# The attention sink of a hybrid decoder kernel as a 129th score column instead of a separate operand

## The chip, the cores and the metric

The kernel runs on one core of a Trainium2 chip. The metric is the device time of one execution in microseconds (us); lower is better. Engines are named as in the profile: PE is TensorE's matrix multiplication and PEld its weight load, DVE is VectorE, ACT is ScalarE, POOL is GpSimd, SP is SyncE, whose queue issues nearly all DMAs.

## What is computed

A trunk of two layers on 512 tokens of width 1024. Each layer has two branches side by side, a gated DeltaNet (8 heads, chunks) and a sliding-window attention (16 query heads on 2 key heads, head width 64, window 128), then an output projection and an MLP of width 4096. The part that the change touches is the attention's softmax with a learned sink per head:

```python
    sink = sinks.astype(jnp.float32).reshape(SW_KV_HEADS, G)[None, None, :, :, None, None]
    m = jnp.maximum(jnp.max(scores, axis=-1, keepdims=True), sink)
    p = jnp.exp(scores - m)
    probs = p / (jnp.sum(p, axis=-1, keepdims=True) + jnp.exp(sink - m))
```

The sink takes part in the maximum and in the sum, and has no value row of its own.

## The kernel before

All large products are done three times over in a split of float32 into a high and a low part (`fp32r`): high by high, low by high, high by low (L339 to L341, L359 to L361, L387 to L389, L400 to L404). Weights come in chunks of 128x1024 by a DMA on SP's queue (`load`, L274), ACT makes the high part (L323) and DVE the low part (L324); `LOOK` = 4 chunks are made ahead and 5 raw buffers are held.

A layer is one long stream of work that a scheduler orders per engine when the program is built: it takes instructions by their place in the program and by its own estimate of when their inputs and buffers are ready, so instructions of different units stand mixed in an engine's queue. Each engine then runs its queue strictly in that order. Only where the program says so (`Order`) is an order written out by hand; of the attention that holds for the four transposes of a group (L919 to L923).

The attention runs in 16 groups per layer (L948), one for each of 4 blocks of 128 tokens (t), 2 key heads (g) and 2 halves (e), and each group has 4 query heads (j). The loop at L959 to L978 issues, for each group, first the units of `MIX` (L46: projections K, G and A of 24 matmuls of 512 columns each; a K unit also does a 128x128 product per chunk and DVE work at L740 to L752), then the first half of `att_group` (L870), then the second half of the group before. In this way a group's softmax has a whole projection unit of matmuls beside it.

First half of a group: scores on PE into PSUM `ps_s` (L892, L893); for t = 0 DVE adds the mask into `M` (L895), else ACT copies the older block's scores (L899) and DVE overwrites those in the band (L900), so that `M` holds 4 heads x 128 scores per token; DVE takes the negated maximum per head (L904, `nm`), the minimum with the negated sink (L905), the difference of the two (L907, `es`); ACT takes exp of that (L908), then four times exp of 128 scores with the row's sum (L910, `den`); DVE adds `es` to `den` (L912) and inverts it (L913); ACT scales the four parts (L916). Second half: four transposes on PE (L922), high part on ACT and low part on DVE (L411, L412 through `split`), two triangular selects on POOL (L932), the product with the values (L938), and the result into `qt` (L941 on ACT, L942 on DVE).

`M` is a 128x512 tile of the pool `T[2]` with four buffers. The negated sinks `nsk` are made once a layer from `snk` (L624 to L628, a DMA on SP and two small DVE instructions). POOL's other work at this time is the rotary embedding (L826 to L831), one power of 128x4 in each K unit (L744), and the selects.

Of the kernel before, what the change touches and what calls it, by code (L numbers as in the profile page):

```python
# [10 lines left out]
F32 = mybir.dt.float32  # L11
# [3 lines left out]
AF = mybir.ActivationFunctionType  # L15
ALU = mybir.AluOpType
AX = mybir.AxisListType
# [3 lines left out]
P = 128  # L21
# [98 lines left out]
def hybrid_trunk(ctx, tc, x, positions, pre_mix_g, dn_conv_w, dn_a_log, dn_dt_bias, dn_norm_g,  # L120
                 sw_sinks, post_mix_g, pre_mlp_g, post_mlp_g, wpk, out, depth=2, dump=None):
    nc = tc.nc
    x = x.rearrange("b s d -> (b s) d")
    out = out.rearrange("b s d -> (b s) d")
# [5 lines left out]
    sm = ctx.enter_context(tc.tile_pool(name="sm", bufs=2))  # L130
# [4 lines left out]
    mm, tr = nc.tensor.matmul, nc.tensor.transpose  # L135
    act, stt = nc.scalar.activation, nc.vector.scalar_tensor_tensor
    tt, ts = nc.vector.tensor_tensor, nc.vector.tensor_scalar
# [3 lines left out]
    def pool_of(tag, bufs):  # L141
        def get(name, dt=F32, n=512):
            return up.tile([P, n], dt, name=name, tag=tag, bufs=bufs)
        return get

    def s1(name, n):
        return sm.tile([P, n], F32, name=name, bufs=1)

    US = pool_of("s", 8)
    T = [pool_of(f"t{i}", 4) for i in range(8)]  # L150
# [8 lines left out]
    def PS(name):  # L159
        return pp.tile([P, 512], F32, name=name, tag="ps")  # L160
# [4 lines left out]
    def PZ(name):  # L165
        return pp.tile([P, 512], F32, name=name, tag="ss", bufs=2)
# [24 lines left out]
    def c4(ap):  # L191
        return ap.rearrange("p (c i) -> p c i", c=4)


    ident = const.tile([P, P], F32, name="ident")
# [214 lines left out]
    def split(src, hi, lo):  # L410
        nc.scalar.copy(hi, src)  # L411
        tt(out=lo, in0=src, in1=hi.bitcast(F32), op=ALU.subtract)  # L412

    def pair(U, name):
        return U(name + "_h", F32R), U(name + "_l", F32R)
# [104 lines left out]
    for l in range(depth):  # L520
# [89 lines left out]
        ps = PS("ps_cw")  # L610
# [11 lines left out]
        dma(dtb, dn_dt_bias[l].partition_broadcast(P))  # L622
        snk = s1("snk", QH)
        dma(snk, sw_sinks[l].partition_broadcast(P))  # L624
        nsk = sm.tile([P, 2, 2, 4], F32, name="nsk", bufs=1)
        for g in range(2):
            ts(out=nsk[:, g], in0=snk[:, g * 8:(g + 1) * 8].rearrange("p (j e) -> p e j", e=2),
               scalar1=-1.0, scalar2=None, op0=ALU.mult)  # L628

        x_res = x if l == 0 else xd  # L630

# [15 lines left out]
        for t in range(NT):  # L647
# [10 lines left out]
           in1=dtb.unsqueeze(2).broadcast_to([P, H, NC]), op=ALU.add)  # L658
# [157 lines left out]
        def att_rope(t):  # L816
            cos, sin = cs[:, t, 0, :], cs[:, t, 1, :]
            for a, nh in ((qt[t], QH), (kv[t][:, 0:128], 2)):
                v = a.rearrange("p (h d) -> p h d", d=HD)
                x1, x2 = v[:, :, 0:HALF], v[:, :, HALF:ROT]  # L820
                cb = cos.unsqueeze(1).broadcast_to([P, nh, HALF])
                sb = sin.unsqueeze(1).broadcast_to([P, nh, HALF])
                rt = T[7]("rt")
                tm = [rt[:, i * P:i * P + nh * HALF].rearrange("p (h d) -> p h d", d=HALF)
                      for i in range(4)]
                ptt(out=tm[0], in0=x1, in1=cb, op=ALU.mult)  # L826
                ptt(out=tm[1], in0=x2, in1=sb, op=ALU.mult)
                ptt(out=tm[2], in0=x2, in1=cb, op=ALU.mult)
                ptt(out=tm[3], in0=x1, in1=sb, op=ALU.mult)
                ptt(out=x1, in0=tm[0], in1=tm[1], op=ALU.subtract)  # L830
                ptt(out=x2, in0=tm[2], in1=tm[3], op=ALU.add)  # L831
# [24 lines left out]
        def att_q(t, g):  # L856
            ps = PS("ps_q")
            for i in range(4):
                j = g * 4 + i
                tr(ps[:, i * P:(i + 1) * P], qt[t][:, j * P:(j + 1) * P], ident)  # L860

            for e in range(2):
                a = T[7]("qT", F32R)
                rh, rl = slice(e * HD, (e + 1) * HD), slice((1 - e) * HD, (2 - e) * HD)
                act(out=a[rh], in_=ps[rh], func=AF.Copy, scale=HD ** -0.5)
                stt(out=a[rl], in0=ps[rh], scalar=HD ** -0.5, in1=a[rh].bitcast(F32), op0=ALU.mult,
                    op1=ALU.subtract)
                at["q", e] = a

        def att_group(t, g, e):  # L870

            if g == 0 and e == 0:
                if t == 0:
                    att_rope(0)
                att_prep(t)
            if (g, e) == (1, 0) and t < NT - 1:
                att_rope(t + 1)
            if e == 0:
                att_q(t, g)
            w0 = max(t - 1, 0) * P  # L880
            qh, den = at["q", e], sm.tile([P, 4], F32, name="den", bufs=4)
            kTh, kTl = kT[g]
            M = T[2]("M")
            for jj in range(2):
                ps = PZ("ps_s")
                pv = ps.rearrange("p (j w) -> p j w", j=2)
                nw = P if t == 0 else 2 * P
                for j in range(2):
                    qs = slice((jj * 2 + j) * P, (jj * 2 + j + 1) * P)
                    kw = slice(w0, w0 + nw)  # L890
                    o_ = pv[:, j, 0:nw]
                    mm(o_, lhsT=qh[:, qs], rhs=kTh[:, kw], start=True, stop=False)  # L892
                    mm(o_, lhsT=qh[:, qs], rhs=kTl[:, kw], start=False, stop=True)  # L893
                Mv = c4(M)[:, jj * 2:jj * 2 + 2, :]
                if t == 0:  # L895
                    tt(out=Mv, in0=pv[:, :, 0:P], in1=ban.unsqueeze(1).broadcast_to([P, 2, P]),
                       op=ALU.add)
                    continue
                nc.scalar.copy(Mv, pv[:, :, 0:P])  # L899
                nc.vector.copy_predicated(  # L900
                    out=Mv, mask=ge.bitcast(I32).unsqueeze(1).broadcast_to([P, 2, P]),
                    data=pv[:, :, nw - P:nw])
            nm = sm.tile([P, 4], F32, name="nm", bufs=4)
            nc.vector.tensor_reduce(out=nm, in_=c4(M), axis=AX.X, op=ALU.max, negate=True)  # L904
            tt(out=nm, in0=nm, in1=nsk[:, g, e, :], op=ALU.min)  # L905
            es = sm.tile([P, 4], F32, name="es", bufs=4)
            tt(out=es, in0=nm, in1=nsk[:, g, e, :], op=ALU.subtract)  # L907
            act(out=es, in_=es, func=AF.Exp)  # L908
            for j in range(4):
                act(out=M[:, j * P:(j + 1) * P], in_=M[:, j * P:(j + 1) * P], func=AF.Exp,  # L910
                    bias=nm[:, j:j + 1], accum_out=den[:, j:j + 1])
            tt(out=den, in0=den, in1=es, op=ALU.add)  # L912
            nc.vector.reciprocal(den, den)  # L913
            for j in range(4):
                js = slice(j * P, (j + 1) * P)
                act(out=M[:, js], in_=M[:, js], func=AF.Copy, scale=den[:, j:j + 1])  # L916
            yield
            ps = PS("ps_pt")
            together = Order(nc.tensor)  # L919
            together.begin()  # L920
            for j in (3, 0, 1, 2):
                tr(ps[:, j * P:(j + 1) * P], M[:, j * P:(j + 1) * P], ident)  # L922
            together.end()  # L923
            pf = pair(T[3], "pf")
            split(ps, *pf)


            pvs = [(at["v", max(t - 1, 0)], 0, a) for a in pf]
            if t > 0:
                for a in pf:  # L930
                    b = T[6]("pc", F32R)
                    nc.gpsimd.affine_select(out=c4(b), in_=c4(a), pattern=[[0, 4], [1, P]],  # L932
                                            compare_op=ALU.is_ge, fill=0.0, base=0,
                                            channel_multiplier=-1)
                    pvs.append((at["v", t], 256, b))
            po = PS("ps_o")
            for i, (v_, o_, a) in enumerate(pvs):
                mm(po, lhsT=v_[:, o_ + g * P:o_ + (g + 1) * P], rhs=a, start=i == 0,  # L938
                   stop=i == len(pvs) - 1)
            o_ = qt[t][e * HD:(e + 1) * HD, g * 512:(g + 1) * 512]  # L940
            nc.scalar.copy(o_, po[HD:P])  # L941
            tt(out=o_, in0=po[0:HD], in1=o_, op=ALU.add)  # L942
# [16 lines left out]
        for i in range(16):  # L959
# [10 lines left out]
            g = att_group(*groups[i])  # L970
# [239 lines left out]
        for m in range(KT):  # L1210
            ps = PM("ps_us")
# [41 lines left out]
        for m in range(4):  # L1253
            ps = (PM, PM, PS, PZ)[m]("ps_ud")
            first.append((ps, mm_a(ps, yT, range(6))))
        mT = []
        for m in range(KT):
# [9 lines left out]
            if m < 4:  # L1267
                ps = first[m][0]
                mm_a(ps, yT, range(6, KT), first[m][1])
            else:  # L1270
                ps = PM("ps_ud")
# [15 lines left out]
        for t in range(NT):  # L1287
            ps = pss[t]
# [72 lines left out]
        for s in range(3):  # L1361
            left = {f"P{i}": [] for i in range(1, 8)}
            raw = [None, None]
            for i, m in enumerate(FF_ORDER):
                if s == 0 and i < 4:
                    ps = early[i][0]
                else:
                    ps = PM("ps_f1")
# [45 lines left out]
        for m in range(8):  # L1414
            ps = PM("ps_f1")
# [21 lines left out]
        else:  # L1437
            for t in range(NT):
                ps = PM("ps_f2")
# [26 lines left out]
```

## Time and profile before

| | us |
|---|---|
| median of 3 runs (1829.16 to 1831.1) | 1830.95 |
| the profiled execution's own time | 1830.59 |
| its span, first to last instruction | 1828.6 |
| PE busy / PEld busy | 1809.1 / 1503.9 |
| DVE busy / ACT busy / POOL busy | 1292.1 / 940.9 / 211.2 |

Busy times are unions of the intervals in which an engine had an instruction under way. Matmuls are pipelined and their ends are modelled, so PE shows as busy over short pauses too; a weight load (PEld) precedes each matmul and its records show such pauses. A wait is put down to the instruction whose semaphore came last.

### The profile page before, as it was taken

Reading aid. Unit: us, or ns where it says so; the run is one execution under the profiler, and the core shown is the slowest. Engines: PE = TensorE matmul, PEld = TensorE weight load, DVE = VectorE, ACT = ScalarE, POOL = GpSimd, SP = SyncE. Lnnn points to the kernel's source line nnn. Section 1 sums busy time; section 2 is a strip of 40 time slices with the busy share of each in tenths; the row PEclk is TensorE's granted clock in tenths of the full one; section 3 lists DMA queues with packets and bytes.
Section 4 is the critical chain, followed back from the end, with each engine's and each line's share of the span. In section 5 each row is a group of like instructions: output and inputs, shape, how many; then the busy total and the mean of one; then the engine's idle time right before and its main releaser. Section 6 shows DMA issues by size and latency. Waiting matters only on the chain.

```text
span 1828.6 us, 26748 instructions
## 1 busy us (share of the span) xinstructions
PE 1809.1 (99%) x9598; PEld 1503.9 (82%) x9598; DVE 1292.1 (71%) x2466; ACT 940.9 (51%) x1913; POOL 211.2 (12%) x386
## 2 busy tenths in 40 slices
PE   9999999999999999999999999999999999999998
PEld 8888778888788888888898887888887898888886
DVE  5499796887566758684556997968885568585934
ACT  6678742444434645544347877234444346554442
POOL 0322102221101000000003221022111010000000
PEclk9999999999999999999999999999999999999999
DMA  5633447554453363564245343485545534544631
GB/s 188 202 118 116 115 149 223 179 170 149 124 191 124 96 216 120 168 217 151 93 151 181 104 127 110 167 234 165 160 139 153 172 119 135 174 163 148 233 102 46
DMA packets 146422, 278.48 MB, mean 152 GB/s; under 512 B 33569, under 2 KB 66657, under 8 KB 146290
## 3 DMA queue, kind: packets, MB, share of 16 engines
q1 hardware_dynamic: 145778, 276.75, 47.4%
q8 instruction: 75, 1.23, 0.3%
q14 instruction: 57, 0.47, 0.1%
q0 software_dynamic: 512, 0.03, 0.0%
HBM read 239.38 MB, written 37.36 MB: 151 GB/s over the span
## 4 chain that ended last, share of the span: by engine, by line
PE 84%; DVE 6%; ACT 5%; DMA 3%; issue 1%; POOL 1%; SPq 0%; POOLq 0%; DVEq 0%; ACTq 0%
PE ps_f L340 6%; PE ps_f L339 6%; PE ps_f L341 6%; PE ps_p L402 3%; PE ps_p L404 3%; PE ps_p L400 3%; PE ps_b L388 3%; PE ps_b L387 3%; PE ps_b L389 3%; PE ps_vp L339 2%; PE ps_us L339 2%; PE ps_ud L339 2%; PE ps_vp L341 2%; PE ps_ud L341 2%; PE ps_ud L340 2%; PE ps_us L340 2%
## 5 line engine op out<-in xcount | busy, mean ns | idle before, releaser
L323 ACT CAST wh<-wr 128x1024 fp32r<-128x1024 f32 (+1 forms) x332 | 343.1, 1040 | 542.2 <-PE ps_f L340 145.8
L324 DVE TENSOR_TENSOR wl<-wr,wh 128x1024 fp32r<-128x1024 f32 (+1 forms) x332 | 400.4, 1216 | 303.6 <-ACT wh L323 300.6
L339 PE MATMUL ps_f<-g_h,wh 128*128 128x512 f32 x448 | 174.3, 389 | 0.0
L340 PE MATMUL ps_f<-g_l,wh 128*128 128x512 f32 x448 | 174.3, 389 | 0.0
L341 PE MATMUL ps_f<-g_h,wl 128*128 128x512 f32 x448 | 174.3, 389 | 0.0
L402 PE MATMUL ps_p<-wl,P_h 128*128 128x512 f32 x336 | 131.4, 391 | 0.4 <-DVE wl L324 0.3
L404 PE MATMUL ps_p<-wh,P_l 128*128 128x512 f32 x336 | 130.8, 389 | 0.0
L400 PE MATMUL ps_p<-wh,P_h 128*128 128x512 f32 x336 | 129.5, 389 | 0.0
L437 POOL TENSOR_TENSOR pr<-pq,pw 128x1 f32<-128x1 f32 x16 | 9.8, 613 | 807.6 <-DVE pq L436 807.6
L339 PEld LDWEIGHTS ps_f<-g_h,wh 128*128 128x128 f32 x448 | 84.1, 188 | 17.4
L341 PEld LDWEIGHTS ps_f<-g_h,wl 128*128 128x128 f32 x448 | 84.1, 188 | 17.4
L340 PEld LDWEIGHTS ps_f<-g_l,wh 128*128 128x128 f32 x448 | 84.1, 188 | 17.4
L402 PEld LDWEIGHTS ps_p<-wl,P_h 128*128 128x128 f32 x336 | 63.1, 188 | 15.8 <-DVE wl L324 2.4
L400 PEld LDWEIGHTS ps_p<-wh,P_h 128*128 128x128 f32 x336 | 63.1, 188 | 13.3
L404 PEld LDWEIGHTS ps_p<-wh,P_l 128*128 128x128 f32 x336 | 63.1, 188 | 12.8
L387 PE MATMUL ps_b<-wh,h_h 128*128 128x432 f32 (+1 forms) x192 | 71.1, 370 | 0.0
L388 PE MATMUL ps_b<-wl,h_h 128*128 128x432 f32 (+1 forms) x192 | 70.5, 367 | 0.3 <-DVE wl L324 0.3
L389 PE MATMUL ps_b<-wh,h_l 128*128 128x432 f32 (+1 forms) x192 | 70.2, 366 | 0.0
L293 DVE TENSOR_TENSOR wr<-wr 128x1024 f32<-128x1024 f32 x48 | 58.0, 1220 | 2.6 <-DMA wr<-in_weights_dram 1.9
L340 PE MATMUL ps_qp<-h_l,wh 128*128 128x512 f32 x128 | 54.0, 422 | 0.0
L339 PE MATMUL ps_vp<-h_h,wh 128*128 128x512 f32 x128 | 53.9, 421 | 0.0
L341 PE MATMUL ps_vp<-h_h,wl 128*128 128x512 f32 x128 | 53.6, 419 | 0.0
(359 smaller groups left out, 4873.6 us busy)
## 6 DMA issues: line engine op xcount, KB each, us to landing
wr<-in_weights_dram SPq DMA_DIRECT2D x320, 512.0 KB, 3.5
wr<-in_weights_dram SPq DMA_DIRECT2D x24, 432.0 KB, 3.6
D<-dd SPq DMA_DIRECT2D x32, 256.0 KB, 3.2
xd<-xo SPq DMA_DIRECT2D x12, 512.0 KB, 2.8
xt<-xd SPq DMA_DIRECT2D x24, 256.0 KB, 3.7
D<-gd SPq DMA_DIRECT2D x16, 256.0 KB, 6.5
dd<-D SPq DMA_DIRECT2D x16, 256.0 KB, 3.9
kkd<-kk SPq DMA_DIRECT2D x16, 256.0 KB, 2.0
```

The source lines that it names most:

```text
L293: tt(out=held[j], in0=held[j], in1=part(i, k, j), op=ALU.add)
L323: nc.scalar.copy(wh[:, :w], wr[:, :w])
L324: sub(out=wl[:, :w], in0=wr[:, :w], in1=wh[:, :w].bitcast(F32), op=ALU.subtract)
L339: mm(ps, lhsT=wh[:, k, :], rhs=hi, start=k == 0, stop=False)
L340: mm(ps, lhsT=wh[:, k, :], rhs=lo, start=False, stop=False)
L341: mm(ps, lhsT=wl[:, k, :], rhs=hi, start=False, stop=k == KT - 1)
L387: mm(pss[t], lhsT=hi[:, tsl], rhs=wh[:, r, :], start=k == 0, stop=False)
L388: mm(pss[t], lhsT=hi[:, tsl], rhs=wl[:, r, :], start=False, stop=False)
L389: mm(pss[t], lhsT=lo[:, tsl], rhs=wh[:, r, :], start=False, stop=k == KT - 1)
L400: mm(pss[t], lhsT=hi[:, c], rhs=wh[:, r, :], start=first, stop=False, skip_group_check=onto)
L402: mm(pss[t], lhsT=hi[:, c], rhs=wl[:, r, :], start=False, stop=False, skip_group_check=onto)
L404: mm(pss[t], lhsT=lo[:, c], rhs=wh[:, r, :], start=False, stop=last, skip_group_check=onto)
```

## The change

`M` gets 129 columns per head. POOL copies the group's four sinks into column 128 ahead of the scores; the maximum (L904) and the four exps with their sums (L910) run over 129 columns, so `nm` and `den` contain the sink. The minimum (L905), the difference (L907), its exp (L908) and the addition (L912) go, and so do `nsk` (L625 to L628) and `es`. The scaling and the transposes take the first 128 columns of each head.

```diff
-        nsk = sm.tile([P, 2, 2, 4], F32, name="nsk", bufs=1)
-        for g in range(2):
-            ts(out=nsk[:, g], in0=snk[:, g * 8:(g + 1) * 8].rearrange("p (j e) -> p e j", e=2),
-               scalar1=-1.0, scalar2=None, op0=ALU.mult)
...
-            M = T[2]("M")
+
+            M = T[2]("M", n=4 * (P + 1)).rearrange("p (j w) -> p j w", j=4)
+            nc.gpsimd.tensor_copy(M[:, :, P], snk[:, g * 8 + e:(g + 1) * 8:2])
...
-                Mv = c4(M)[:, jj * 2:jj * 2 + 2, :]
+                Mv = M[:, jj * 2:jj * 2 + 2, 0:P]
...
-            nc.vector.tensor_reduce(out=nm, in_=c4(M), axis=AX.X, op=ALU.max, negate=True)
-            tt(out=nm, in0=nm, in1=nsk[:, g, e, :], op=ALU.min)
-            es = sm.tile([P, 4], F32, name="es", bufs=4)
-            tt(out=es, in0=nm, in1=nsk[:, g, e, :], op=ALU.subtract)
-            act(out=es, in_=es, func=AF.Exp)
+            nc.vector.tensor_reduce(out=nm, in_=M, axis=AX.X, op=ALU.max, negate=True)
             for j in range(4):
-                act(out=M[:, j * P:(j + 1) * P], in_=M[:, j * P:(j + 1) * P], func=AF.Exp,
-                    bias=nm[:, j:j + 1], accum_out=den[:, j:j + 1])
-            tt(out=den, in0=den, in1=es, op=ALU.add)
+                act(out=M[:, j], in_=M[:, j], func=AF.Exp, bias=nm[:, j:j + 1], accum_out=den[:, j:j + 1])
             nc.vector.reciprocal(den, den)
             for j in range(4):
-                js = slice(j * P, (j + 1) * P)
-                act(out=M[:, js], in_=M[:, js], func=AF.Copy, scale=den[:, j:j + 1])
+                act(out=M[:, j, 0:P], in_=M[:, j, 0:P], func=AF.Copy, scale=den[:, j:j + 1])
...
-                tr(ps[:, j * P:(j + 1) * P], M[:, j * P:(j + 1) * P], ident)
+                tr(ps[:, j * P:(j + 1) * P], M[:, j, 0:P], ident)
```

## Rows read from the trace of the kernel before

**Rows 1.** The page: span, busy time of each engine, granted clock in 40 slices.

```profile
span 1828.6 us, 26748 instructions
...
PE 1809.1 (99%) x9598; PEld 1503.9 (82%) x9598; DVE 1292.1 (71%) x2466; ACT 940.9 (51%) x1913; POOL 211.2 (12%) x386
...
PEclk9999999999999999999999999999999999999999
```

**Rows 2.** Busy time by engine: layer 1's attention, an MLP stretch, layer 2's attention.

```profile
80.00:240.00 160.00, 157.48 (x810) 127.58 (x809) 138.56 (x408) 125.66 (x376) 34.33 (x58) 1.00 0.36 110
540.00:700.00 160.00, 159.79 (x812) 136.17 (x811) 102.77 (x129) 83.77 (x135) 5.67 (x8) 1.00 0.41 136
985.00:1145.00 160.00, 157.12 (x811) 127.49 (x810) 137.99 (x407) 125.32 (x373) 35.10 (x60) 1.00 0.36 111
```

Columns: from:to, length, then busy us and instructions of PE, PEld, DVE, ACT, POOL, then PE's granted clock, DMA share, GB/s.

**Rows 3.** Waits for the scaled scores: whole span, then from 80 to 240 us.

```profile
PE ps_pt L922 <- ACT M L916: 3.9, 6, 0.8
...
PEld ps_pt L922 <- ACT M L916: 9.5, 15, 1.2
...
PE ps_pt L922 <- ACT M L916: 2.0, 3, 0.8
```

Columns: who waited for whom: us in total, times, longest us.

**Rows 4.** Timeline of one group's softmax (the third of layer 1), DVE, ACT, PE.

```profile
101.92 0.68 DVE L904 TENSOR_REDUCE nm<-M 128x4 f32<-128x512 f32 x1
...
102.72 0.16 DVE L905 TENSOR_TENSOR nm<-nm,nsk 128x4 f32<-128x4 f32 x1
...
103.01 0.16 DVE L907 TENSOR_TENSOR es<-nm,nsk 128x4 f32<-128x4 f32 x1
...
103.60 0.19 ACT L908 ACTIVATE es<-es 128x4 f32<-128x4 f32 x1
103.70 0.39 ACT L910 ACTIVATE M<-M,nm 128x128 f32<-128x128 f32 x1
...
104.98 0.16 DVE L912 TENSOR_TENSOR den<-den,es 128x4 f32<-128x4 f32 x1 [0.21 <-ACT M L910]
...
105.73 1.28 ACT L916 ACTIVATE M<-M,den 128x128 f32<-128x128 f32 x4 [0.59 <-DVE cj L747]
...
107.06 0.66 PE L922 MATMUL ps_pt<-ident,M 128*128 128x128 f32 x4 [0.75 <-ACT M L916]
```

**Rows 5.** DVE and ACT by group of instructions: the ones removed.

```profile
L907 DVE TENSOR_TENSOR es<-nm,nsk 128x4 f32<-128x4 f32 x32 | 6.0, 188 | 0.1
L905 DVE TENSOR_TENSOR nm<-nm,nsk 128x4 f32<-128x4 f32 x32 | 5.9, 185 | 0.2
...
L912 DVE TENSOR_TENSOR den<-den,es 128x4 f32<-128x4 f32 x32 | 5.0, 157 | 7.2 <-ACT M L910 7.2
...
L908 ACT ACTIVATE es<-es 128x4 f32<-128x4 f32 x32 | 6.2, 195 | 1.3 <-DVE es L907 1.1
```

Columns: line, engine, operation, out<-in with shapes, count | busy us, mean ns of one | idle us before it and what ended it.

**Rows 6.** Durations of two lines of DVE: reads 1 to 3 elements off, and aligned.

```profile
L714 DVE SCALAR_TENSOR_TENSOR kk<-ps_kp,cw,kk x48: 717/741/751, 87.2 to 1085.4; 128x509 f32<-128x509 f32 x16, 128x510 f32<-128x510 f32 x16, 128x511 f32<-128x511 f32 x16
...
L718 DVE SCALAR_TENSOR_TENSOR kk<-th,kk x16: 656/691/695, 90.4 to 1087.6; 128x512 f32<-128x512 f32 x16
```

Columns: line, engine, operation, out<-in, count: shortest/median/longest ns, first and last start in us; shapes.

**Rows 7.** Small instructions of POOL, and the selects, by group.

```profile
L213 POOL MEMSET pw<- 128x4 f32 x1 | 0.1, 97 | 0.0
...
L830 POOL TENSOR_TENSOR kv<-rt 128x16 f32<-128x16 f32 x8 | 3.8, 481 | 0.2
...
L932 POOL TENSOR_SCALAR_AFFINE_SELECT pc<-pf_h 128x512 fp32r<-128x512 f32 x24 | 16.2, 675 | 122.9 <-ACT pf_h L411 122.9
```

**Rows 8.** Timeline: a select on POOL and a small DVE instruction beside it.

```profile
151.48 0.64 POOL L932 TENSOR_SCALAR_AFFINE_SELECT pc<-pf_h 128x512 fp32r<-128x512 f32 x1 [5.16 <-ACT pf_h L411]
...
151.52 0.61 DVE L742 TENSOR_SCALAR ssk<-ssk 128x4 f32<-128x4 f32 x1
```

**Rows 9.** The sinks' DMA and the waits of SP's queue for weight buffers.

```profile
L624 SPq DMA_DIRECT2D snk<-in_sw_sinks_dram x2: 328/328/328, 12.7 to 19.6; - x2
...
SPq L274 <- DVE wl L324: 641.6, 212, 13.2
```

Columns of the first: count, shortest/median/longest ns, start of the first and the last in us.

## The prediction

> **What bounds the kernel.** The page comes first: of a span of 1828.6 us PE is busy 1809.1, at full clock in every slice [rows 1]. So time changes only where PE's order of work gets a pause shorter or longer; work removed from DVE or ACT is worth nothing by itself. The second view is busy time by stage, for the two stretches in which the 16 attention groups of a layer run, with an MLP stretch beside them [rows 2]. By PE's own column the attention stretches have 160 - 157.48 = 2.5 and 160 - 157.12 = 2.9 us of idle time, 5.4 in all. DVE is the busiest of the others there, 138.56 and 137.99 of 160 (87%), against 102.77 in the MLP stretch: the softmax's small instructions stand in a queue that is nearly full.
>
> PE's column hides short pauses, since its ends are modelled. The weight loads show them: 136.17 us of loading in the MLP stretch against 127.58 and 127.49 in the attention, for nearly the same number of instructions [rows 2]. The differences are 8.6 and 8.7 us, 17.3 in all. Part of that is another mix of shapes, so I take 17.3 as an upper bound on what PE loses in both stretches and 5.4 as a lower one. The Trainium skill ("Trainium Kernel Development and Optimization", section Performance Expectations) says that matmul busy time is a bad measure and that the share of LDWEIGHTS is a good one; by that rule alone the room is 17.3 and not 5.4. No term of the forecast rests on it; it weighs only in the second rival.
>
> The third view is the waits. PE waits for the end of a group's scaling six times, 3.9 us in all and 0.8 at most, and PEld 15 times for 9.5 [rows 3]. Three of the six lie in the first layer, so three in the second, and they sum to 2.0 us in the first [rows 3]. One of them is written out in the timeline [rows 4]: maximum at 101.92, minimum with the sink at 102.72, difference at 103.01, exp of the sink at 103.60 between the first and the second exp of the scores, addition at 104.98, scaling from 105.73, transposes at 107.06 after PE had stood idle 0.75 us.
>
> **The change, step by step.** *Removed on DVE:* three instructions of 128x4 in each of 32 groups, means 185, 188 and 157 ns [rows 5], 0.53 us a group, 17.0 us in all; the four for `nsk` lie outside the groups and are as small. Two of the three lie in the chain: the minimum (before the exps) and the addition (after them). The difference runs beside the first exp. In the undisturbed case each is worth 0.16 us [rows 4], so 0.32 of the chain.
>
> *Removed on ACT:* one exp of 128x4, 195 ns by the mean [rows 5]. It stands in the run of exps; in the timeline it starts at 103.60 and the next instruction at 103.70 [rows 4], so it delays the run by 0.10 and at most by 0.19. I take 0.15, between the two.
>
> *Widened:* the maximum reads 516 elements for 512. At 0.68 us for 512 that is at most 0.68 x 4/512 = 5 ns more; each exp takes one element more, at most 0.39/128 = 3 ns, four of them 12 ns [rows 4]. Together 0.02 us a group. The heads' parts of `M` now start 516 bytes apart, not 512, for the masked writes, the exps, the scaling and PE's transposes. No row shows that layout. The nearest are the convolution's instructions, which read and write 1 to 3 elements off the tile's start: median 741 ns, against 691 for a like one that is aligned [rows 6], so 0 to 7% more. I take 0, since a head's part is read and written at one and the same offset; at 7% the eight ACT instructions would cost 8 x 0.39 x 0.07 = 0.2 us a group and take almost half of the gain.
>
> *Added on POOL:* 32 copies of 128x4. The trace has none of that shape: the nearest below is a fill of 128x4 at 97 ns, the nearest above a two-input instruction of 128x16 at 481 [rows 7], so 3.1 to 15.4 us of POOL in all. Less than nothing it can't cost, as it only adds work. I take 0.2 each, nearer the fill because of the equal size. POOL is busy only 34.33 of 160 us [rows 2]. The copy needs only the sinks, loaded long before, and a free buffer of `M`; with four buffers that is the one whose last reader is the transposes four groups earlier. So it can run a group or more ahead of the maximum, and I cost it at nothing. What covers it is this lead; if it ran just ahead of the maximum, it would add 0.1 to 0.5 us plus the wait in POOL's queue.
>
> A POOL instruction can also hold DVE: beside a select of 0.64 us a DVE instruction of 128x4 took 0.61, and both ended at about 152.12 [rows 8]; the others of this size take 157 to 188 ns [rows 5]. So 32 copies can take at most 15.4 of the freed 17.0 us away again, and by the fill's price 3.1. The Trainium skill ("GPSIMD Engine Reference", section Specifications) says that GpSimd shares its SBUF interfaces with VectorE and that the two contend for some kinds of DVE instructions; that speaks against the change, and this row agrees. I weigh it as less freed DVE time, not as a loss in the chain.
>
> *Moved:* the sinks of the second layer. Their DMA was issued at 19.6 us [rows 9], since `nsk` had freed the tile. Now `snk` is read until the last copy of the first layer, so this DMA stands later in SP's queue, behind a wait for POOL, and weight loads stand behind it. SP already waits 641.6 us in all for weight buffers [rows 9], and the sinks are needed only in the stretch that begins at 985 us [rows 2]; I take nothing for it, and at most one pause as long as PE's longest for the scaling, 0.8 us [rows 3].
>
> **Sum.** Each of the six groups in which PE waits gets a chain shorter by 0.32 + 0.15 - 0.02 = 0.45 us in the undisturbed case, and somewhat more where the removed DVE instructions are slower (means 0.19 for 0.16): I take 0.5. Of a mean wait of 3.9/6 = 0.65 that much goes: 6 x 0.5 = 3.0 us. What is late next is ACT: four exps and four scalings stay and make the rest. The other 26 groups give nothing, since PE has a projection's matmuls to do until they are ready. Against the profiled execution's 1830.59 this is 1827.6; that one lies 0.36 under the median of the runs shown, so against the median 1830.95 - 3.0 = **1828.0 us**, 0.16% faster. 0.2%, 3.7 us, is about what a measurement of this kernel can tell from no change, so this counts as the same, just inside: faster begins at 1827.3, slower at 1834.6.
>
> **Rivals.**
> - *Hidden or replanned, no change.* The scheduler places the transposes by when it thinks the softmax ends; with a shorter chain it places them earlier, and PE waits as often. For it: PE already waits in so few groups that they are deviations from a plan. Against: removed instructions can't run late. 1831.0 (1830 to 1832).
> - *DVE is the real limit of the stretch.* Then not only the six waits shrink; 17.0 us freed in 276.6 us of DVE work (6%) lets score evacuations, splits and weight preparations run earlier too. The pauses are 5.4 to 17.3 us; if a third of the larger goes, 5.8 us: 1825.2. For it: 87% busy. Against: DVE waits for ACT too, ACT is at 125.66/160 = 79% itself, and POOL's copies may take part of it back. All of 5.4 to 17.3 would be 1825.6 to 1813.7, which I don't believe.
> - *Slower: transposes set too early.* The new plan gives another order in the 16 groups, the same in both layers, so each misplacement costs twice. Place: the transposes in PE's queue, before the end of ACT's scaling, with the projection's matmuls queued behind them. Price: a mean wait of 0.65. Now three groups a layer have it; five more would cost 10 x 0.65 = 6.5: 1837.5. It shows as slower from six further groups on (3.9 us).
> - *Slower: the copy is late.* If POOL's queue holds a group's copy behind the selects of the group before, the maximum waits for that group's transposes and ACT's split; the selects wait 122.9 us in all for `pf_h` [rows 7]. At 0.5 us for each of the 24 groups with selects: 12 us, 1843. Against: the lead of four buffers.
>
> **How the numbers follow.** Chances: forecast 0.36 (its own range 1826 to 1830), no change 0.22, DVE limit 0.22, transposes early 0.15, copy late 0.05. Faster by over 0.2%: 0.10 of the forecast, 0.21 of the DVE case, 0.02 of no change, 0.33. Slower: 0.12 of the early transposes and 0.05 of the late copy, 0.17. The rest, 0.50, is the same. The range runs from 1822, which leaves out the far end of the DVE case, to 1836, which leaves out the worse half of the early transposes and the late copy.
>
> **What would show it.** Right: DVE's busy time in both stretches down by 12 to 17 us in all; PE's waits for the scaling under 1.5 us; copies of 0.1 to 0.5 us that end long before their maximum; no DVE wait for POOL at the maximum. Wrong: waits for the scaling as many or more (replanned), waits of the maximum for POOL (late copy), exps and scalings longer than 0.39 us (the 516-byte steps), or pauses in other places, of the scores, the value products or the weights.

## The result, and the profile after

The changed kernel takes 1839.44 us (median of 6 runs, 1838.12 to 1841.76) against 1830.12 for the kernel before on the same chip: a ratio of 1.005 with a 95% interval of 1.0039 to 1.0062, **9.3 us slower**. The forecast was 3.0 us faster, and the range ended at 1836.

The page of the changed kernel (span, busy time by engine, granted clock) answers to [rows 1]:

```profile
span 1837.0 us, 26616 instructions
...
PE 1813.2 (99%) x9598; PEld 1503.4 (82%) x9598; DVE 1289.1 (70%) x2366; ACT 939.3 (51%) x1881; POOL 215.6 (12%) x418
...
PEclk9999999999999999999999999999999999999999
```

The instructions are as planned: 100 fewer on DVE, 32 fewer on ACT, 32 more on POOL. The clock is full. PE has the same 9598 matmuls and is busy 4.1 us longer, which no removed wait explains: first sign that its matmuls themselves ran at another pace.

Busy time by stage, the windows and columns of [rows 2]:

```profile
80.00:240.00 160.00, 156.56 (x807) 126.92 (x806) 135.12 (x356) 123.89 (x355) 36.75 (x70) 1.00 0.37 114
540.00:700.00 160.00, 159.78 (x809) 136.00 (x808) 100.59 (x128) 82.38 (x132) 5.67 (x8) 1.00 0.42 140
985.00:1145.00 160.00, 156.49 (x812) 127.42 (x811) 132.16 (x349) 123.33 (x351) 39.11 (x79) 1.00 0.36 113
```

DVE was relieved by 3.4 and 5.8 us in the attention stretches (by the page, 3.0 over the whole span), and PE is busy a little less there, not more (156.56 for 157.48, 156.49 for 157.12). The MLP stretch, which the change doesn't touch, does three matmuls fewer in its 160 us.

The waits over the whole span, which answer to [rows 3]; the columns are us in total, times, longest:

```profile
PE ps_pt L913 <- ACT M L907: 5.1, 7, 1.2
...
PEld ps_pt L913 <- ACT M L907: 11.8, 16, 1.6
...
POOL M L881 <- PE ps_pt L913: 64.8, 15, 8.9
```

Waits for the scaling grew from 3.9 to 5.1 us. The last row is the new copy, waiting at the head of POOL's queue for the buffer of `M`.

The same group as in [rows 4], in the timeline of the changed kernel:

```profile
101.85 0.69 DVE L902 TENSOR_REDUCE nm<-M 128x4 f32<-128x516 f32 x1
102.59 0.40 ACT L904 ACTIVATE M<-M,nm 128x129 f32<-128x129 f32 x1
...
104.43 0.17 DVE L905 RECIPROCAL den<-den 128x4 f32<-128x4 f32 x1
...
104.64 1.28 ACT L907 ACTIVATE M<-M,den 128x128 f32<-128x128 f32 x4 [0.22 <-DVE den L905]
...
105.97 0.66 PE L913 MATMUL ps_pt<-ident,M 128*128 128x128 f32 x4 [1.11 <-ACT M L907]
```

From the maximum to the transposes it takes 4.12 us where it took 5.14, so the chain did get shorter, by more than forecast; how much of that the removed instructions made, and how much the new order of the queues, is a question for the experiments. But PE stood idle 1.11 us before the transposes instead of 0.75. Its last matmul ahead of them ended 1.45 us earlier (104.86 for 106.31): the transposes had been set earlier in PE's queue by more than the chain gained. Over all 32 groups the median from the start of the maximum to the end of the scaling went from 6.19 to 4.37 us. In the built program's order 112 of the 128 transposes stand, on average, 10 PE instructions further ahead.

The new and the widened instructions, and the sinks' DMA (count, shortest/median/longest ns, first and last start):

```profile
L881 POOL COPY M<-snk x32: 179/190/460, 17.5 to 1096.9; 128x4 f32<-128x4 f32 x32
...
L902 DVE TENSOR_REDUCE nm<-M x32: 678/684/691, 82.9 to 1139.1; 128x4 f32<-128x516 f32 x32
...
L904 ACT ACTIVATE M<-M,nm x128: 386/392/424, 83.6 to 1141.0; 128x129 f32<-128x129 f32 x128
...
L907 ACT ACTIVATE M<-M,den x128: 385/389/412, 85.9 to 1142.9; 128x128 f32<-128x128 f32 x128
...
L624 SPq DMA_DIRECT2D snk<-in_sw_sinks_dram x2: 328/330/332, 13.0 to 187.7; - x2
```

The copy costs 190 ns, the reduce and the exps what they did, and the 516-byte steps nothing. The second layer's sinks are loaded at 187.7 us, not at 19.6 [rows 9].

So where are 9.3 us? The distances between matmuls give the first suspect. In `ps_us`, a projection behind the attention with 192 matmuls of 512 columns a layer and hardly a wait, PE of the kernel before starts one every 226 or 227 ns, the first few of a layer apart. In the changed kernel the distances go 224 to 238, in a pattern that repeats every 24 matmuls. The disturbance starts at the eighth of each 24, which is the first that reads a tile of the ring `T[2]` at an odd place: `M`'s 516 floats stretch all four slots of that ring, and other tiles use them too. I add up, over all 512-column matmuls of the trace, the distance from one start to the next less 226.67 ns, leaving out distances of 255 and more (those hold a wait), and call that **the pace**: it is time lost, so less is better. It is 7.17 us before and 12.24 after: 5.1 of the 9.3. The largest parts of the 5.1 are in `ps_us` (1.6), in the products of `ps_p` (1.5) and in `ps_b` (1.1).

### The profile page after: what moved, and what is told of

It reads as the page before. It is cut to its first block, busy times and chain, and to the rows that moved or that the text cites. A ratio compares the mean times of both kernels' runs of the same rounds, so it can differ in the third digit from the quotient of the medians.

```text
span 1837.0 us, 26616 instructions
## 1 busy us (share of the span) xinstructions
PE 1813.2 (99%) x9598; PEld 1503.4 (82%) x9598; DVE 1289.1 (70%) x2366; ACT 939.3 (51%) x1881; POOL 215.6 (12%) x418
## 4 chain that ended last, share of the span: by engine, by line
PE 86%; DVE 5%; ACT 4%; DMA 2%; issue 1%; POOL 1%; SPq 0%; DVEq 0%; POOLq 0%; ACTq 0%
PE ps_f L340 6%; PE ps_f L339 6%; PE ps_f L341 6%; PE ps_p L402 4%; PE ps_p L400 4%; PE ps_p L404 4%; PE ps_b L387 3%; PE ps_b L388 3%; PE ps_b L389 3%; PE ps_vp L339 2%; PE ps_vp L341 2%; PE ps_vp L340 2%; PE ps_us L341 2%; PE ps_us L340 2%; PE ps_us L339 2%; PE ps_ud L339 2%
## 5 line engine op out<-in xcount | busy, mean ns | idle before, releaser
L904 ACT ACTIVATE M<-M,nm 128x129 f32<-128x129 f32 x128 | 49.9, 394 | 8.7 <-DVE nm L902 8.6
```

## Experiments

Three theories: *address* (the slots' starting addresses cost PE pace), *order* (the scheduler dealt the queues anew, and the new order is worse), *column* (copies and rows of 129 cost by themselves). Each run has its own kernel-before runs on the same chip; differences are against those.

### First set

**padded_after**

```diff
-            M = T[2]("M", n=4 * (P + 1)).rearrange("p (j w) -> p j w", j=4)
+            M = T[2]("M", n=528)[:, :4 * (P + 1)].rearrange("p (j w) -> p j w", j=4)
```

> The changed kernel with M allocated 528 floats wide (2112 bytes, a multiple of 64) of which it uses 516; every engine's order is that of the changed kernel. Three theories of the 9.3 us (1839.44 against 1830.12). Address: M's 516 floats put the four slots of its ring 2080 bytes apart, so that slots 1 and 3 begin at a multiple of 64 bytes where all other operands of TensorE begin 32 above one, and 512-column matmuls lose pace after reading them; in the trace of the changed kernel the intervals over 226.67 ns sum to 12.24 us, before to 7.17. Order: the scheduler, seeing a shorter chain, set the transposes ahead of more matmuls, and TensorE waits for them. Column: the copies and the rows of 129 cost by themselves. Address expects 1839.4 less 5.1, so 1834.4 (1833.4 to 1835.4), and the ps_us matmuls back at 226 to 227 ns each. Order alone, or column alone, expects 1839.4, with 231 to 232 ns in ps_us.

Measured: 1837.18 against 1831.48, +5.7 us (ratio 1.0032, 1.0021 to 1.0044). The pace fell only from 12.24 to 9.88, and `ps_us` kept 1.20 of its 1.68. The address was at work, but "multiples of 64" was the wrong rule: every slot now begins 32 above one.

**shifted_before**

```diff
-            M = T[2]("M")
+            M = T[2]("M", n=516)[:, :512]
```

> The kernel before with M allocated 516 floats wide of which it uses 512: nothing else of the program changes, neither an instruction nor an engine's order, only the addresses of the slots of T[2] and of the rings behind it. Address expects 1830.1 and 5.1, so 1835.2 (1834.2 to 1836.2), with ps_us at 231 to 232 ns a matmul on average. Order and column both expect 1830.1, within 0.8.

Measured: 1836.78 against 1831.48, +5.3 us (1.0029, 1.0017 to 1.004), pace 12.10. Not one instruction and not one place in a queue differs from the kernel before; only addresses do. That settles that the slots cost about 5 us by themselves. The row of `ps_us`' high-by-high matmuls in the first layer, in the kernel before and then in this run:

```profile
L339 PE MATMUL ps_us<-oT_h,wh x64: 389/389/470, 246.2 to 289.2; 128*128 128x512 f32 x64
```

```profile
L339 PE MATMUL ps_us<-oT_h,wh x64: 387/395/467, 246.5 to 290.4; 128*128 128x512 f32 x64
```

First to last start 43.0 us before, 43.9 here. Each matmul is recorded 6 ns longer in the median, and the view names the same waits in both runs.

**padded_old_order**: the padded kernel, held to the kernel before's order by dependencies between neighbours in each queue.

```diff
+    for eng, n_, text in (
...
+        for a_, b_ in zip(seq, seq[1:]):
+            tc.add_manual_dep(b_, a_.name, mybir.DependencyInfo(
+                mybir.DependencyClass.NoSync, mybir.DependencyReason.DATA), reason="order")
```

> The changed kernel with M padded to 528 floats, and TensorE, VectorE, ScalarE and GpSimd held to the order of the kernel before by dependencies written out (the 32 copies fall between GpSimd's instructions where the scheduler puts them). Address and order together expect no more than 1830.1, and, where the shorter chain takes half a microsecond off six waits as forecast, 1827 to 1829. If the chain is not shorter on the chip, 1830. Column expects over 1832, because the copies and wide rows are all still there.

Measured: 1833.12 against 1831.48, +1.6 (1.001, 1.0001 to 1.0019), pace 9.85. The old order takes back 4 of the padded kernel's 5.7 us. By its expectation, "over 1832", this spoke for *column*; but 2.7 us of pace are still missing.

**before_new_pe_order**: the kernel before, held in the same way to the changed kernel's order, for PE alone.

> The kernel before, its sink still taken in by the four small operations and M 512 wide, with TensorE alone held to the order that it has in the changed kernel; VectorE and ScalarE are scheduled to suit. Order expects a loss at least as large as the 9.3 less 5.1 that the addresses leave, about 4 us, since the chain behind each transpose is longer here: 1834 to 1842, with more waits of ps_pt for the scaling than the 6 and 15 of the kernel before. Address and column expect 1830.1, within 0.8, if the waits don't matter.

Measured: 1863.76 against 1831.48, +32.3 (1.0176, 1.0162 to 1.019), where 4 to 12 us were expected. Its waits:

```profile
PE ps_pt L928 <- ACT M L922: 19.9, 14, 2.8
...
PEld ps_pt L928 <- ACT M L922: 26.9, 16, 3.2
```

PE's new order needs the new chain: with the four small operations still in the chain (its median is 6.07 us) the waits for the scaling are five times as long, 16 us more. That is half of the loss. The run prices a mixture that neither kernel runs, so only its sign is used.

### Second set: which addresses

Starting addresses of the ring's four slots modulo 256 (what is left on division by 256), in bytes, as the programs allocate them, and the pace in us (`ps_ud` is the other branch's projection, none of whose operands lies in `T[2]` or behind it):

```
kernel              bytes apart   modulo 256          ps_us  ps_ud  ps_b   all
before              2048          160 160 160 160     0.04   0.04   0.00   7.17
changed             2080          160 192 224   0     1.68   0.04   1.14  12.24
shifted_before      2080          160 192 224   0     1.78   0.04   1.13  12.10
padded_after        2112          160 224  32  96     1.20   0.03   0.80   9.88
before_stride_2176  2176          160  32 160  32     0.35   0.05   0.77   9.28
before_stride_2304  2304          160 160 160 160     0.01   0.05   0.00   6.63
before_stride_2560  2560          160 160 160 160     0.06   0.06   0.00   6.91
before_all_at_32    2048           32  32  32  32     0.05   0.04   0.00   6.83
before_all_at_0     2048            0   0   0   0     0.05   0.04   0.00   6.53
```

Of the rings of large tiles one lies behind `T[2]`: `T[3]`. At 2080 bytes apart it is moved too, to 32 where the other large tiles lie at 160; in all other rows it begins as they do. So the two rows of 2080 mix more than the slots of `T[2]`.

**before_stride_2176**: `n=544` in the edit of shifted_before.

> The kernel before with M allocated 544 floats (2176 bytes) and 512 of them used; orders unchanged. The padded kernel spoke against multiples of 64: its slots all begin 32 above one, and its ps_us matmuls still lose 1.20 us. What all 512-column operands of the kernel before share is the remainder 416 on division by 2048. Here the slots of T[2] are all alike modulo 128 (32) but not modulo 256 or more. If remainders modulo 128 decide, the time is that of before and the intervals over 226.67 ns sum to 7.2 us; if a larger modulus decides, they sum to 9 to 12 us, and the time is 2 to 5 us above before.

Measured: 1832.8 against 1831.23, +1.6 (1.0009, 1.0 to 1.0018), pace 9.28: the pace in the range for a larger modulus, the time a little under it. Alike modulo 128 is not enough.

**before_stride_2560**: `n=640`, and for room:

```diff
-            gT = sm.tile([32, P], F32, name="gT", bufs=1)
+            gT = sm.tile([32, P], F32, name="gT", tag="z1", bufs=1)
...
```

> The kernel before with M allocated 640 floats (2560 bytes) and 512 used; the room for it is found by letting five small tiles (gT, egT, ang, kk_, gc) share the room of others; orders unchanged. Slots are alike modulo 512, not modulo 1024 or 2048. If 512 or less decides: the time of before within 0.8 us, sum 7.2 us. If the full 2048 decides: 9 to 12 us in the sum, 2 to 5 us above before. If the size of the ring by itself were the cost, above before as well.

Measured: 1831.2 against 1831.23 (1.0001, 0.9993 to 1.001), pace 6.91. A larger ring costs nothing; slots alike modulo 512 cost nothing.

**before_stride_2304**: `n=576`.

> The kernel before with M allocated 576 floats (2304 bytes), 512 used, the five small tiles sharing room as in before_stride_2560; orders unchanged. A stride of 2176 left the four slots at 32, 160, 288 and 416 modulo 512 and the intervals over 226.67 ns at 9.28 us; 2560 left them all at 416 modulo 512 and the sum at 6.91. Here two slots lie at 416 and two at 160: alike modulo 256, not modulo 512. If 256 decides: 6.9 to 7.2 us, 0.1 or less of it in ps_us, and the time of before within 0.8 us. If 512 decides: 8 to 9.5 us, and 1 to 2 us above before.

Measured: 1830.88 against 1831.28 (0.9998, 0.9989 to 1.0007), pace 6.63, of which `ps_us` has 0.01:

```profile
L339 PE MATMUL ps_us<-oT_h,wh x64: 388/390/472, 245.6 to 288.5; 128*128 128x512 f32 x64
```

Alike modulo 256 is enough here. What stayed open was whether the slots must be *alike* or must lie at a *good value* such as 160, since the runs so far changed both at once.

**before_all_at_32** and **before_all_at_0**: a constant tile ahead of all large tiles grows by 128 (or, with 32 floats, 96) bytes and takes them all along.

```diff
-    pw = const.tile([P, 8], F32, name="pw")
+    pw = const.tile([P, 40], F32, name="pw")[:, 0:8]
```

> The kernel before with 128 more bytes in a constant tile (pw, 40 floats of which 8 are used) that lies ahead of all large tiles: every large tile then begins at 32 modulo 256 where it began at 160; orders unchanged. If it is likeness that counts, the pace stays at 6.6 to 7.2 us and the time within 0.8 us of before. If 160 is a good place and 32 a bad one, pace is lost in every 512-column matmul, not only in those that read T[2]: with 4.4 ns each as in ps_us of the changed kernel, over 10 us.

> The same with 96 bytes: every large tile begins at a multiple of 256. Likeness: pace 6.6 to 7.2 us, time within 0.8 us of before. Value: lost pace, or a gain if 0 is a better place than 160; then also in ps_kp, ps_vp and ps_f, whose matmuls hardly read T[2].

Measured: 1831.89 and 1831.11 against 1831.79 (1.0001, 0.9992 to 1.001, and 0.9997, 0.9988 to 1.0006), pace 6.83 and 6.53. Likeness counts, not the value.

### What the order costs, and what the change gives

**after_stride_2560**: the changed kernel with `n=640` and the same room.

> The changed kernel, its own orders, M in slots of 2560 bytes. If 512 or less decides, the padded kernel's remaining pace (9.88 less 7.17 = 2.7 us) goes, and its +5.7 against before becomes +3.0 (2 to 4): that is what the order by itself costs. If not, +5 to +7.

Measured: 1834.59 against 1831.23, +3.4 (1.002, 1.0011 to 1.0029), pace 6.79: as expected.

**old_order_stride_2560**: padded_old_order with `n=640`.

> The changed kernel in slots of 2560 bytes, with TensorE, VectorE, ScalarE and GpSimd held to the order of the kernel before. The padded one in this order stood at +1.6 with 9.85 us in the sum of pace; less 2.7 that is -1.0 (-2.0 to 0) against before, which would be the change as it was forecast, without its two side effects. If the copies or the rows of 129 cost by themselves it stays above before.

Measured: 1832.85 against 1831.23, +1.6 (1.0009, 1.0001 to 1.0018), though the pace fell to 6.42. A miss, and the trace says why. Set against before_stride_2560 stage by stage, this run is 0.65 us ahead by 197 us, then loses 3.0 us at one place, and wins 1.6 us in the second layer's attention. A wait of SP's queue, and then the engines' waits from 180 to 216 us:

```profile
SPq L625 <- POOL M L882: 6.3, 1, 6.3
```

```profile
PE ps_pt L915 <- ACT M L909: 3.2, 1, 3.2
ACT M L909 <- DVE den L907: 3.2, 1, 3.2
DVE tmp L795 <- DMA ub<-ud: 3.0, 1, 3.0
```

SP's queue stands at the second layer's sinks until POOL's last copy has read the first layer's. The load of `ub` behind it leaves at 196.3 us (193.3 in before_stride_2560). DVE waits for `ub` with the reciprocal behind it, ACT waits for the reciprocal, PE for ACT.

**old_order_sinks_twice**: a second buffer for the sinks.

```diff
-        snk = s1("snk", QH)
+        snk = sm.tile([P, QH], F32, name="snk", bufs=2)
```

> The changed kernel in slots of 2560 bytes and in the order of the kernel before, with two buffers instead of one for the loaded sinks. In the run without that, SP's queue stood 6.3 us at the DMA of the second layer's sinks until the last copy on GpSimd, the load of ub behind it was issued at 196.3 us where the kernel before issued it at 193.3, VectorE waited 3.0 us for it, and TensorE 3.2 us at ps_pt behind VectorE. Outside that stall the run gained on before_stride_2560: 0.9 us in the first attention and 1.6 in the second. Queue theory: the stall goes and the time is 1.6 + 2.5 lower than 1832.85 less what repeats, so 1828.7 (1827.7 to 1830), below the kernel before. If the copies and the wide rows cost by themselves: 1832 to 1833, as without it.

Measured: 1829.53 against 1830.82, **-1.3 us** (0.9994, 0.9985 to 1.0002). The stall is gone and 2.9 us with it. The two loads, then the wait for the scaling over the whole span:

```profile
L780 SPq DMA_DIRECT2D ub<-ud x1: 360/360/360, 192.0 to 192.0; - x1
...
L625 SPq DMA_DIRECT2D snk<-in_sw_sinks_dram x2: 328/382/435, 12.6 to 19.1; - x2
```

```profile
PE ps_pt L915 <- ACT M L909: 2.0, 4, 0.7
```

*Column* falls with this run: all copies and wide rows are in it. Its interval still takes in 1, so this version, the best of all here, is not shown to beat the kernel before. But it has the kernel before's order on PE, so the two traces can be set side by side matmul by matmul: against before_stride_2560 it wins 0.9 us from 80 to 200 us and 0.9 from 985 to 1145, about what its waits for the scaling lost (3.9 less 2.0).

It also shows what the removed instructions are worth by themselves. The median from the start of the maximum to the end of the scaling is 6.00 us here, against 6.19 in the kernel before. The group of [rows 4] in the timeline of this run:

```profile
101.75 0.68 DVE L904 TENSOR_REDUCE nm<-M 128x4 f32<-128x516 f32 x1
...
102.42 0.58 ACT L934 COPY qt<-ps_o 64x512 f32<-64x512 f32 x1 [0.27 <-PE ps_o L931]
...
103.03 0.41 ACT L906 ACTIVATE M<-M,nm 128x129 f32<-128x129 f32 x1
...
104.92 0.17 DVE L907 RECIPROCAL den<-den 128x4 f32<-128x4 f32 x1
...
106.46 0.66 PE L915 MATMUL ps_pt<-ident,M 128*128 128x128 f32 x4 [0.33 <-ACT M L909]
```

and the place of the first exp and the reciprocal in the kernel before:

```profile
102.59 0.58 ACT L941 COPY qt<-ps_o 64x512 f32<-64x512 f32 x1 [0.26 <-PE ps_o L938]
...
103.20 0.40 ACT L910 ACTIVATE M<-M,nm 128x128 f32<-128x128 f32 x1
...
105.47 0.17 DVE L913 RECIPROCAL den<-den 128x4 f32<-128x4 f32 x1
```

From the start of the maximum to the first exp it is 1.28 us in both: that exp stands behind a copy into `qt` in ACT's queue, so the minimum, done at 102.88, had not been what it waited for. From the first exp to the reciprocal it is 1.89 us for 2.27, with the addition and the exp of the sink gone. PE waits 0.33 us where it waited 0.75. In the first group of a layer nearly nothing is won (a wait of 0.66 for 0.72): its first exp stands behind a cast of weights on ACT in both runs, and its reciprocal behind another group's maximum on DVE.

**after_sinks_twice**: the same buffer and slots with the changed kernel's own order on all engines but SP.

> The changed kernel in slots of 2560 bytes, its own orders on all engines but SP, with two buffers for the sinks. There the first wait for ub took 0.7 us, so the queue theory expects 0 to 1 us less than the 3.4 above before of the run without it: +2.4 to +3.4. The rest is then the order. If the sinks' DMA was the whole of it: 0.

Measured: 1834.74 against 1830.82, +3.9 (1.0022, 1.0013 to 1.0031), a little above the range. In this order the sinks' DMA was not the cost. Its waits, to be set beside the row above:

```profile
PE ps_pt L913 <- ACT M L907: 5.6, 8, 1.3
...
PEld ps_pt L913 <- ACT M L907: 10.6, 14, 1.7
```

These two runs have the same instructions and the same addresses and differ in the order of the queues alone (SP's too): 1834.74 - 1829.53 = **5.2 us for the order**, of which 5.6 - 2.0 = 3.6 is waiting at the transposes. In the two traces the loss lies in the two attentions, 2.6 us from 80 to 240 us and 2.7 from 985 to 1200. What makes up the other 1.6 was not followed further.

**pe_old_sinks_twice**: that kernel with PE alone in the kernel before's order.

> The same kernel, slots of 2560 bytes and two buffers for the sinks, with TensorE alone held to the order of the kernel before; the other engines are scheduled to suit. If it is the place of the transposes and products in TensorE's order that costs, the time is that of the run with four engines held, 1828.7 (1827.7 to 1830.5). If it is VectorE's and ScalarE's order, it stays near the changed kernel's +2.4 to +3.4 above before.

Measured: 1847.24 against 1830.82, +16.4 (1.0088, 1.0074 to 1.0101), outside both expectations. The waits for the scaling are nearly gone, but:

```profile
PE ps_o L931 <- ACT pf_h L412: 4.9, 4, 1.7
PE ps_o L931 <- DVE pf_l L413: 4.7, 8, 1.3
```

With before_new_pe_order this says that the four queues are one plan. The loss of 5.2 us belongs to the plan; it can't be put down to PE's queue or to DVE's and ACT's. The median chain fits that: 6.19 us before, 6.07 with the four operations kept and DVE and ACT planned anew (before_new_pe_order), 6.00 without them in the old order, 4.37 without them in the new one (after_sinks_twice) and 4.23 here. It takes the removal and the new plan together to make it short. Why the scheduler plans as it does, and whether the removed instructions or the added copies make it do so, no run shows.

## Why the prediction was wrong

The parts close: slots +5.3 (shifted_before), plan +5.2 (the two runs above), the change itself -1.3 (old_order_sinks_twice), together +9.2 for a measured +9.3. Each has an uncertainty of about 2 us, so that the sum closes to a tenth is luck.

- **The step that failed first is "Widened".** It priced the 516-element tile from the inside: longer reads, 516-byte steps within `M`. Both were right at nothing (684 ns against 0.68 us, exps of 392 and scalings of 389 ns). It never asked what the size does to the *addresses* of the slots, which `oT`, `mT`, `h3` and others share with `M`. That was worth +5.3 us, in stretches that the change doesn't touch, and no bound or rival covered it; only the last sign of being wrong, "pauses in other places", came near it.
- **The step that failed second is the sum's premise that PE's order holds.** Six waits of PE, each shorter by 0.5 us: that needs the transposes to stay where they are. Rival "transposes set too early" had the mechanism (0.15) and the signs: earlier transposes in nearly all groups, waits longer, the same in both layers. Its 1837.5 took ten waits more, of 0.65 us each; measured is 5.2 us for the plan, with one wait more in the changed kernel (seven) and two in after_sinks_twice (eight), and longer ones, up to 1.3 us. The rival "no change" had the other half of the reasoning: a scheduler that aims the transposes at the end of the chain gives a shorter chain back.
- **The forecast's mechanism shows in the waits, and its size was too large.** With order and addresses held, the waits fell from 3.9 us in six [rows 3] to 2.0 in four, and the time by 1.3 us (by the interval between 2.7 less and 0.4 more), where the sum had 3.0. The term that failed is the 0.32 for DVE, worked out for an "undisturbed case": in a full queue it is not the case. The minimum gave nothing in the group of [rows 4], because the first exp stood behind a copy in ACT's queue that ended at 103.17, as the kernel before's own timeline shows; the addition gave more there than its 0.16; and the first group of each layer won next to nothing. In the changed kernel the chain shrank by 1.8 us in the median, not by 0.45, but only 0.2 of that comes without the new plan.
- **DVE as the real limit** fell: DVE was relieved by 9.3 us in both stretches (12 to 17 had been named) and nothing came of it; in old_order_sinks_twice, where DVE is busy 8.9 us less over the whole span (1283.2 for 1292.1), the time moved by 1.3. The Trainium skill's rule ("Trainium Kernel Development and Optimization", section Performance Expectations) that the weight loads' share is a good measure of how close a kernel is to its limit said no more here than the time itself: PEld went from 1503.9 to 1503.4 us, so its share fell, from 82.2 to 81.8%, only because the span grew.
- **The copy** cost 190 ns, as taken. It did wait in POOL's queue, 64.8 us in all, but no DVE instruction waited for a copy, and PE waited for a select once, 0.5 us (once and 0.2 in the kernel before).
- **"Moved"** named the right queue, SP's, behind a wait for POOL. Its bound of 0.8 us was too low: in the old order that wait cost 2.9 us of the time. In the changed kernel's own order it cost nothing measurable.

## What to carry to other kernels

A tile's size sets the addresses of every tile that shares its ring or lies behind it; when a change widens one, look at where the slots begin before and after, and test it alone by widening the tile without using it. A kernel whose queues a scheduler orders has a second variable in every edit: hold the order while you price the edit. An instruction taken out of a chain is worth its time only where the next one was not held by a neighbour in its own queue: look there before you add it up. And when a buffer's last reader moves to a later engine, give its next load a buffer of its own, or the whole DMA queue waits with it.

## What the runs showed of the hardware that was not expected

PE's 512-column matmuls of `ps_us`, `ps_ud` and `ps_b` ran at 226.7 to 226.8 ns from start to start where the operands' tiles all began alike modulo 256 (at 160, at 32 or at 0), and at 231.0 on average in the changed kernel's `ps_us`, where `T[2]` and `T[3]` mixed them (1.68 us over 384 matmuls is 4.4 ns each). In padded_after the pace took several matmuls to recover after one that read from such a slot (233, 226, 236, 228, 232, 231 ns, then 227); in before_stride_2176 one distance alone was long (234). It holds for the operand that moves (`ps_us`) and for the one that is loaded as weights (`ps_b`, 1.14 us, where parts of `mT` and `h3` lie in `T[2]` and `T[3]`; 0.80 in padded_after, with `T[3]` in its place). Why it is so, no run here shows. The Trainium skill ("SBUF — State Buffer", section Operand start alignment) lets a float32 operand begin at any multiple of 4 bytes and says that its runs timed nothing; in time, these runs differ by 5 us between 2080 and 2560 bytes apart.
